# Expert inputs fetched by rows with an indirect DMA and transposed, in place of one-hot products; eight weight buffers in place of five

## The chip, the core and the metric

One core of a Trainium2 chip runs the whole kernel in one launch. The metric is the device time in microseconds of one execution. Engines are named as in the profile: PE (TensorE, the matrix engine), DVE (VectorE), ACT (ScalarE), POOL (GpSimd), SP (SyncE, which here only issues DMAs). Transfers between the chip's DRAM and the on-chip SBUF run on 16 DMA engines, whichever engine issues them.

## What is computed

Two transformer blocks over 512 tokens of width 1024, everything in float32. The first block (two layers with recurrence, retention and spatial gating) and the attention of the second are not touched. The second block ends in a mixture of 32 experts, of which each token takes 4:

```python
def moe_ffn(h, w_router, b_router, w_gate_up, b_gate_up, w_down, b_down):
    logits = jnp.dot(h, w_router) + b_router
    top_logit, top_idx = lax.top_k(logits, TOP_K)        # TOP_K = 4 of N_EXPERTS = 32
    gate = jax.nn.softmax(top_logit, axis=-1)
    ...
    def expert_block(args):
        tok, g, e = args
        xb = h_pad[tok]                                  # rows of the tokens of expert e
        gu = xb @ w_gate_up[e] + b_gate_up[e]            # 1024 -> 2 x 1024
        y = clamped_swiglu(gu) @ w_down[e] + b_down[e]   # 1024 -> 1024
        return y * g[:, None]
    ...
    out = jnp.zeros((n_tok + 1, d), y.dtype).at[slot_tok].add(y.reshape(n_slots, d))
```

Then `x + gt2 * moe_ffn(h2)` is normalized and written out. An expert has a matrix of 1024 x 2048 and one of 1024 x 1024, 12 MB; 32 of them are 384 MB, each read once.

## The kernel before

Products run in a 1-pass float32 format of the matrix engine. To keep the accuracy, each operand is split into a high and a low part: ACT copies the value into the short format (`hi`), DVE subtracts that from the value (`lo`), both in `split` (L278 to L280), and a product is the sum of three, hi x hi, lo x hi and hi x lo.

The first 1.27 ms are the dense part; the expert stage follows. It starts with `router` (L1020 to L1149): logits, the choice of four, the position of each pair among those of its expert (`pos`), and four values per pair (`vals`: token, filled, gate in two parts). Its last loop (L1136 to L1148) makes the scaled and shifted rows of the tokens in four quarters of 256 columns, `raw`, and splits each into `hn` (two tiles, 16 KB per partition each), where all rows stay in SBUF for the whole stage.

`moe` (L1468) then goes through the experts in order. One expert has up to 128 slots (`CAP`). `gate_up(e, hf)` makes one half of the gate columns (`pg`) and of the linear ones (`pl`) in four weight tiles, each with 12 products of 512 columns; `act_rows` transposes the activations of a half (4 transposes by PE, then a split); `down(e, hf)` multiplies them with two tiles of the second matrix (`pd`). Order: `gate_up(e, 0)`, `down(e-1, 1)`, `gate_up(e, 1)`, `down(e, 0)`. Behind `down(e, 1)` the result is scaled by the gate and `accumulate` (L1213) adds its rows to `x_rows` in DRAM, an indirect DMA issued by POOL; empty slots have an index out of bounds and move nothing.

`gather(e0)` (L1281) prepares the inputs of two experts, e0 and e0+1. DVE makes a one-hot matrix `oh` (512 tokens x 256 slots) from `pos`; PE multiplies both parts of all rows with it: for each of 4 pairs of 128-column chunks and each of 2 parts, 8 products of 256 columns into one PSUM tile `xT`, which ACT copies into `x`, already transposed. Then a small product with `vals` ("slot") and two small transposes ("slotT") give the token index and the gate of each slot (`slot_columns`, L1200). It is a generator with four parts; `moe` calls the next part in the last tile (t == 3) of each `gate_up`, so that the inputs for experts e+2 and e+3 are made while e and e+1 run. Gather 0 runs ahead of the loop.

`wsplit` (L1218) loads one weight tile of 1 MB (128 x 2048 f32) with a DMA issued by SP and splits it. The landing tiles take turns in five buffers (`wsts`, i % 5), the hi and lo tiles in three each. A scheduler orders the instructions of each engine when the program is built, by priorities and its own estimates; on the chip each engine runs them in that order and waits on semaphores.

Of the kernel before, what the change touches and what calls it, by code (L numbers as in the profile page):

```python
# [26 lines left out]
# ------------------------------------------------------------------ layout  # L27
# [27 lines left out]
# order in which the column chunks of w_in are used: LRU input, LRU gate, retention, spatial gating  # L55
# [101 lines left out]
    # experts: [e][tile][p][...] with each tile one run per partition; four tiles of two row chunks for each  # L157
    # half of the gate columns beside the like half of the linear ones, then four tiles of w_down
# [6 lines left out]
    # constants of the shapes  # L165
# [26 lines left out]
# ------------------------------------------------------------------ kernel  # L192

class Kern:
# [6 lines left out]
    # tiles of one tag are handed out in program order, so each role has its own  # L201
# [16 lines left out]
    # ---- weights of the dense part, in the order of their use; splits run ahead as far as the buffers reach  # L218
# [43 lines left out]
    def weights(self, key, m=128, held=0):  # L262
        """the next weights, (hi, lo); held: how many before them are still in use"""
# [19 lines left out]
    # ---- 1 / sqrt(x * scale + eps) of a few columns, by Newton steps  # L283
# [14 lines left out]
    def colsum(self, *sq, nblk=4):  # L298
        """sum over partitions of [128, nblk * 128] -> PSUM [128 (token in block), nblk]"""
# [7 lines left out]
    def bcast(self, nat, out, nblk=4, p=None):  # L307
        """[128 (token in block), nblk] -> [128, nblk * 128], every partition the same row"""
# [6 lines left out]
    def row_bcast(self, cols, out):  # L315
        """[128, 8] columns of a feature vector -> two [128, 512], every partition the vector"""
# [27 lines left out]
    def lru_scale(self):  # L344
        """-8 * softplus(-lambda), and 4 * softplus(-lambda)"""
# [23 lines left out]
    def rope_tables(self):  # L369
        """cos and signed sin of positions * inv, [128, T], both halves of the head alike"""  # L370
# [31 lines left out]
    # ---- rms norm of self.h: y = h * g split; 1 / rms goes in where products leave PSUM  # L402
# [25 lines left out]
    def square_sum(self, ss, h, k, scale=1.0, n=T):  # L428
        """ss = sum over k of (h * scale) ** 2"""
# [8 lines left out]
    def proj(self, w, y, nk=DC, p=None, between=()):  # L438
        """one chunk of 128 output features for all tokens -> PSUM; between: what goes between its products"""
# [8 lines left out]
    def projs(self, keys, y, ws=()):  # L448
        """three chunks side by side, so that none waits for the last rows of y; ws: weights that are there"""
# [8 lines left out]
    def silu_gate(self, l, c, y, rs):  # L458
        """g * sigmoid(g) of chunk c"""
# [8 lines left out]
    def gated(self, o, gs):  # L468
        """o * gs, split"""
# [5 lines left out]
    # ---- recurrent branch, group g of three chunks  # L475
    def lru_group(self, l, g, y, rs):
# [41 lines left out]
        # sqrt(1 - a^2) = (1 + a) sqrt(tanh(-log(a) / 2))  # L518
# [13 lines left out]
    def rope(self, p, hi, lo, tabs):  # L532
        """rotated chunk, split"""
# [11 lines left out]
    # ---- retention branch, heads 2 * hp and 2 * hp + 1  # L545
# [72 lines left out]
    # ---- spatial gating branch  # L618
# [73 lines left out]
    def layer(self, l):  # L692
# [32 lines left out]
        # per-layer embedding  # L725
# [35 lines left out]
    # ---- block 2: modulation of both conditions, as columns; each call is half the rows for 512 columns  # L761
# [37 lines left out]
    def modcols(self, name, gain, j, o):  # L799
        """gain * (1 + scale); scale is the modulation of condition j at column o"""  # L800
# [6 lines left out]
    def modulated(self, src, a, b, bc, t, yh, yl):  # L807
        """(src * a) * bc + b, split; a and b are columns"""
# [6 lines left out]
    def headnorm(self, p, n):  # L815
        """1 / rms over the 128 features of a head -> [128, n] rows"""
# [7 lines left out]
    def context(self):  # L824
        """modulated context, split"""
# [20 lines left out]
    def context_kv(self):  # L846
        nc = self.nc
        # keys of a head: (hi, lo) of the tokens, then (hi, lo) of the context; values: six blocks of keys
# [36 lines left out]
    def block2(self):  # L885
# [3 lines left out]
        # final norm of block 1 and first norm of block 2: with A = mean(h^2) + eps, the product of both  # L889
        # 1 / rms is 1 / sqrt(mean((h g)^2) + eps A)  # L890
# [16 lines left out]
        # tables of the axial rotation with the gains of q and k  # L907
# [19 lines left out]
        # short convolution; the scores of the first head between its last products  # L927
# [29 lines left out]
        # attention  # L957
# [13 lines left out]
    def scores(self, q, kv, P, early=False):  # L971
        """softmax of one head: four blocks of queries by rows, keys (tokens, context)"""
# [46 lines left out]
    # ---- second norm, router, slots of the experts; stops before each chunk of the residual and at the end  # L1019
    def router(self):  # L1020
# [10 lines left out]
        # bias of the logits: b_router + w_router.T @ shift  # L1031
# [13 lines left out]
        # triangle and ones for the counts, and four columns that stand for the choices beyond the fourth  # L1045
# [9 lines left out]
        for k in range(8):  # L1055
# [12 lines left out]
            # tokens by rows  # L1068
# [31 lines left out]
        # choices of the tokens  # L1100
# [3 lines left out]
        # position of each pair among those of its expert  # L1104
# [176 lines left out]
    def gather(self, e0):  # L1281
# [8 lines left out]
        for j in range(4):  # L1290
# [12 lines left out]
            if j < 3:  # L1303
                yield
# [359 lines left out]
```

## Time and profile before

| | |
|---|---|
| median of three runs | 2576.26 us (2575.6 to 2578.38) |
| profiled execution, first to last instruction | 2573.3 us |
| PE busy | 2521.1 us, 98% |
| DVE busy | 2030.0 us, 79% |
| ACT busy | 1403.1 us, 55% |
| POOL busy | 145.4 us, 6% |
| DMA | 553.92 MB, mean 215 GB/s |
| clock granted to PE, mean | 0.994 of full speed |

The profile lists instructions with the line that made them, the tile written and the tiles read. "PEld" is the load of a product's fixed operand and runs beside the products. Busy times of neighbouring matrix products overlap, since they are pipelined; how fast they follow each other is seen in their start times. A line can be that of a helper: all splits stand under L279 (ACT) and L280 (DVE), so they are told apart by their tiles. The stage of the experts begins at about 1270 us, and from about 1320 to 2540 us every pair of experts looks alike.

### The profile page before, as it was taken

How to read it: one execution, taken by the hardware profiler on the slowest of the kernel's cores; microseconds unless marked ns; L12 is line 12 of the kernel's file. 1: busy time of each engine (PE TensorE's matmuls, PEld its weight loads, DVE VectorE, ACT ScalarE, POOL GpSimd, SP SyncE). 2: the span in 40 equal slices, each digit the busy share in tenths (PEclk: the TensorE clock that was granted, in tenths of full speed). 3: DMA queues.
4: the chain of work that ended last, by engine and by line, in shares of the span. 5: the costliest groups of instructions: out<-in, count | busy, mean ns of one | idle time of the engine just before them, and what ended most of it. 6: DMA issues, size and time to landing. Idle time of an engine off the chain costs nothing. (4 is left out here: it accounts for less than half of the span.)

```text
span 2573.3 us, 31850 instructions
## 1 busy us (share of the span) xinstructions
PE 2521.1 (98%) x12331; PEld 2042.9 (79%) x12331; DVE 2030.0 (79%) x2582; ACT 1403.1 (55%) x1469; POOL 145.4 (6%) x85
## 2 busy tenths in 40 slices
PE   8999999999999999999899999999999999999997
PEld 6778878777788787887678888888888888888885
DVE  8866757578576577868788888888888888888897
ACT  6523324345233245334666666666666666666665
POOL 0000000000000000000210101101001011010013
PEclk9999999999999999999899999999999999999998
DMA  4243242422423433220288888888898888888886
GB/s 161 82 142 99 82 163 95 139 97 90 153 83 101 162 118 131 66 92 17 107 325 335 320 334 316 324 338 318 324 330 320 331 318 317 338 327 317 330 325 242
DMA packets 104525, 553.92 MB, mean 215 GB/s; under 512 B 13872, under 2 KB 14256, under 8 KB 55216
## 3 DMA queue, kind: packets, MB, share of 16 engines
q1 hardware_dynamic: 94368, 532.85, 56.7%
q0 software_dynamic: 5248, 10.64, 2.0%
q10 hardware_dynamic: 4752, 8.34, 1.0%
q8 instruction: 99, 1.62, 0.3%
q14 instruction: 58, 0.48, 0.1%
HBM read 539.18 MB, written 20.97 MB: 218 GB/s over the span
## 5 line engine op out<-in xcount | busy, mean ns | idle before, releaser
L279 ACT ACTIVATE wh<-w 128x2048 fp32r<-128x2048 f32 (+2 forms) x571 | 923.3, 1619 | 694.5 <-PE pd L1375 196.5
L280 DVE TENSOR_TENSOR wl<-w,wh 128x2048 fp32r<-128x2048 f32 (+2 forms) x571 | 1092.8, 1924 | 223.1 <-ACT wh L279 221.1
L1335 PE MATMUL pg<-wh,x 128*128 128x512 f32 x1024 | 411.0, 401 | 0.0
L1336 PE MATMUL pl<-wh,x 128*128 128x512 f32 x1024 | 404.8, 395 | 0.0
L274 PE MATMUL prj<-ty,wh 128*128 128x512 f32 x880 | 349.6, 397 | 11.3 <-ACT wh L279 8.5
L275 PE MATMUL prj<-ty,wh 128*128 128x512 f32 x880 | 347.7, 395 | 1.1 <-DVE ty L812 0.8
L276 PE MATMUL prj<-ty,wl 128*128 128x512 f32 x880 | 346.4, 394 | 1.1 <-DVE wl L280 1.1
L1335 PEld LDWEIGHTS pg<-wh,x 128*128 128x128 f32 x1024 | 192.7, 188 | 44.6 <-ACT x L1300 0.7
L1336 PEld LDWEIGHTS pl<-wh,x 128*128 128x128 f32 x1024 | 192.8, 188 | 43.0
L1335 PE MATMUL pg<-wl,x 128*128 128x512 f32 x512 | 202.8, 396 | 1.9 <-DVE wl L280 1.9
L274 PEld LDWEIGHTS prj<-ty,wh 128*128 128x128 f32 x880 | 166.4, 189 | 48.1 <-ACT wh L279 9.8
L1336 PE MATMUL pl<-wl,x 128*128 128x512 f32 x512 | 202.2, 395 | 0.0
L276 PEld LDWEIGHTS prj<-ty,wl 128*128 128x128 f32 x880 | 166.2, 189 | 37.9 <-DVE wl L280 2.5
L275 PEld LDWEIGHTS prj<-ty,wh 128*128 128x128 f32 x880 | 166.1, 189 | 35.7 <-DVE ty L812 1.8
L1215 POOL DMA_INDIRECT x_rows<-ye,si x32 | 105.3, 3292 | 1123.5 <-DVE ye L1383 1123.5
L1375 PE MATMUL pd<-wl,ah 128*128 128x512 f32 x512 | 165.6, 400 | 0.0
L1375 PE MATMUL pd<-wh,al 128*128 128x512 f32 x512 | 161.7, 397 | 0.0
L1375 PE MATMUL pd<-wh,ah 128*128 128x512 f32 x512 | 161.1, 396 | 0.0
L274 PE MATMUL prj<-tmix,wh 128*128 128x512 f32 x320 | 127.1, 398 | 0.4 <-ACT tmix L279 0.4
L275 PE MATMUL prj<-tmix,wh 128*128 128x512 f32 x320 | 126.5, 395 | 0.0
L276 PE MATMUL prj<-tmix,wl 128*128 128x512 f32 x320 | 126.0, 394 | 0.0
L1335 PEld LDWEIGHTS pg<-wl,x 128*128 128x128 f32 x512 | 96.3, 188 | 26.1 <-DVE wl L280 2.7
(440 smaller groups left out, 3736.3 us busy)
## 6 DMA issues: line engine op xcount, KB each, us to landing
w<-in_wgu SPq DMA_DIRECT2D x256, 1024.0 KB, 5.4
w<-in_wdn SPq DMA_DIRECT2D x128, 1024.0 KB, 7.0
w<-in_w SPq DMA_DIRECT2D x118, 512.0 KB, 3.4
wa<-in_wada SPq DMA_DIRECT2D x48, 512.0 KB, 3.4
w<-in_wob SPq DMA_DIRECT2D x32, 384.0 KB, 3.1
w<-in_wg SPq DMA_DIRECT2D x16, 512.0 KB, 3.5
w<-in_wos SPq DMA_DIRECT2D x8, 512.0 KB, 3.3
w<-in_wo SPq DMA_DIRECT2D x8, 512.0 KB, 3.3
```

Source lines behind the costliest of these rows:

```text
L274: mm(ps, a[0], b[0], start=first, stop=False)
L275: mm(ps, a[0], b[1], start=False, stop=False)
L276: mm(ps, a[1], b[0], start=False, stop=last)
L279: ins = self.nc.scalar.activation(hi, src, AF.Copy).ins
L280: self.nc.vector.tensor_sub(lo, src, hi.bitcast(F32))
L1215: self.nc.gpsimd.indirect_dma_start(out=self.x_d[:, :], out_offset=self.rows(idx), in_=y, in_offset=None, bounds_check=T - 1, oob_is_err=F ...
L1335: nc.tensor.matmul(pg, x[k], w[:, s, 0], start=first, stop=False)
L1336: nc.tensor.matmul(pl, x[k], w[:, s, 1], start=first, stop=False)
L1375: nc.tensor.matmul(self.pd[n], a[:, k], w[:, s, n * 512:(n + 1) * 512], start=hf == 0 and k == 0 and a is ah and w is wh, stop=hf == 1 and ...
```

## The change

All scaled rows go to DRAM: in `router`, each quarter of `raw` is stored into `h_rows` and no longer split, and `hn` is gone. `gather(e0)` first makes the slots' indices and gates, then POOL issues two indirect DMAs that fetch the rows of each expert, 4 KB per filled slot, into two landing tiles `xg` (zeroed once; an empty slot keeps what it held). The next two parts, one for each expert, transpose its rows with PE in two groups of four 128x128 blocks, and `split` makes the two parts from PSUM (ACT and DVE). The one-hot matrix stays for the indices. The generator has three parts in place of four, and in `moe` the calls for the first two experts are as for the others, from the second half of expert 0 on. In the space of `hn` stand three more landing buffers for weights: eight in turn (i % 8). In `overflow`, which runs only where an expert has over 128 pairs, the rows need not be put together again. Comments and doc strings are cut too.

```diff
@@ router
             for b in range(0 if j else 4):
-                nc.scalar.activation(r[:, b], r[:, b], AF.Copy, scale=nat[:, b:b + 1])
+                self.scaled = nc.scalar.activation(r[:, b], r[:, b], AF.Copy, scale=nat[:, b:b + 1]).ins
...
-                ins = self.split(r, *(x[:, :, j * 256:j * 256 + 256] for x in self.hn))
-            if j == 0:
-                self.scaled = ins
+            nc.sync.dma_start(self.h_d.rearrange("(b p) c -> p b c", p=128)[:, :, j * 256:j * 256 + 256], r)
@@ rows_pools
-        rows = self.ctx.enter_context(pool("mrows", 1))
-        self.hn = [rows.tile([128, 4, D], F32R, name=f"hn{x}") for x in "hl"]
-        self.wsts = [self.moe_pools.enter_context(pool("mw", 1))]
+        self.xgp = self.moe_pools.enter_context(pool("mxg", 2))
+        self.wsts = 3 * [self.moe_pools.enter_context(pool("mwa", 3))]
+        self.wsts += [self.moe_pools.enter_context(pool("mw", 1))]
@@ wsplit
-        w = self.wsts[i % 5].tile([128, 2048], F32, name="w", tag="w", bufs=3 if 0 < i % 5 < 4 else 1)
+        w = self.wsts[i % 8].tile([128, 2048], F32, name="w", tag="w", bufs=1 if i % 8 in (3, 7) else 3)
@@ gather
+        ahead = 0 if e0 else AHEAD
+        xg = []
+        for q in range(2):
+            xg.append(self.xgp.tile([128, D], F32, name="xg", tag="xg"))
+            if e0 == 0:
+                nc.gpsimd.memset(xg[q], 0.0)
+        with tc.high_priority(ahead):
             self.hot = nc.vector.tensor_tensor(oh, ...
...            (slot, slotT and slot_columns, moved here from the end)
+                nc.gpsimd.indirect_dma_start(out=xg[q], out_offset=None, in_=self.h_d[:, :],
+                                             in_offset=self.rows(self.idx[e0 + q]),
+                                             bounds_check=T - 1, oob_is_err=False)
+        yield
         for q in range(2):
             self.xs[e0 + q] = [], []
-        for j in range(4):
-            for i in range(2):
-                p = self.trp("xT")
-                for s in range(2):
-                    k = 2 * j + s
-                    for b in range(4):
-                        nc.tensor.matmul(p[:, s * 256:(s + 1) * 256], self.hn[i][:, b, k * 128:(k + 1) * 128], oh[:, b],
-                                         start=b == 0, stop=b == 3)
-                t = (self.xp if e0 % 4 else self.hpool).tile([128, 2, 2, 128], F32R, name="x", tag="h", bufs=8)
-                with self.tc.high_priority(0 if e0 else AHEAD):
-                    nc.scalar.activation(t.rearrange("p s q c -> p (s q c)"), p, AF.Copy)
-                for q in range(2):
-                    self.xs[e0 + q][i].extend(t[:, s, q] for s in range(2))
-            if j < 3:
-                yield
+            with tc.high_priority(ahead):
+                for hf in range(2):
+                    p = self.trp("xT")
+                    for k in range(4):
+                        c = (4 * hf + k) * 128
+                        nc.tensor.transpose(p[:, k * 128:(k + 1) * 128], xg[q][:, c:c + 128], self.ident)
+                    pool = self.xp if e0 % 4 else self.hpool
+                    t = [pool.tile([128, 4, 128], F32R, name="x", tag="h", bufs=8) for _ in range(2)]
+                    self.split(p.rearrange("p (k s) -> p k s", k=4), *t)
+                    for i in range(2):
+                        self.xs[e0 + q][i].extend(t[i][:, k] for k in range(4))
+            yield
@@ moe
-                    for _ in range((t == 3) * (0, 1, 2, 1)[2 * e + hf] if e < 2 else t == 3):
+                    if t == 3 and e + hf:
                         next(g, None)
```

## Rows read from the trace of the kernel before

**Rows 1.** The page's chain that ended last: shares of the span by line.
```profile
PE pd L1375 14%; PE pg L1335 14%; PE pl L1336 14%; PE xT L1296 4%; PE aT L1359 1%; PE pl L1339 1%; PE pg L1339 1%; PE slot L1307 0%; PE slotT L1313 0%; DVE xr L1436 0%; DVE wl L280 0%; ACT fsq L1423 0%; DVE xr L1422 0%; DVE rx L290 0%; PE fx L1419 0%
```
**Rows 2.** Busy times, one pair: length, engines (instructions), PE clock, DMA share, GB/s.
```profile
1716.00:1795.00 79.00, 79.00 (x383) 64.74 (x382) 69.01 (x51) 53.87 (x42) 6.70 (x2) 1.00 0.89 326
```
**Rows 3.** Instructions of ACT in order (start, duration): the slot copy, three pairs apart.
```profile
1438.63 0.36 ACT L1310 ACTIVATE slr<-slot 8x256 f32<-8x256 f32 x1
...
1676.15 0.36 ACT L1310 ACTIVATE slr<-slot 8x256 f32<-8x256 f32 x1
```
**Rows 4.** Instructions of PE in order, merged runs counted: transposes, products, one gather call.
```profile
1707.22 0.60 PE L1359 MATMUL aT<-ident,li 128*128 128x128 f32 x4
1707.58 0.48 PE L1335 MATMUL pg<-wh,x 128*128 128x512 f32 x1
1707.89 0.40 PE L1336 MATMUL pl<-wh,x 128*128 128x512 f32 x1
...
1713.03 0.40 PE L1336 MATMUL pl<-wl,x 128*128 128x512 f32 x1
1713.26 1.07 PE L1296 MATMUL xT<-oh,hnh 128*128 128x256 f32 x8
1714.17 1.07 PE L1296 MATMUL xT<-oh,hnl 128*128 128x256 f32 x8
1715.08 0.39 PE L1339 MATMUL pg<-bias,sel 128*128 128x512 f32 x1
```
**Rows 5.** Groups by line and shape, 1300 to 2540: busy us, mean ns, idle before.
```profile
L280 DVE TENSOR_TENSOR wl<-w,wh 128x2048 fp32r<-128x2048 f32 x376 | 857.5, 2294 | 141.4 <-ACT wh L279 139.9
...
L280 DVE TENSOR_TENSOR al<-aT,ah 128x512 fp32r<-128x512 f32 x63 | 43.1, 684 | 0.4 <-ACT ah L279 0.4
```
**Rows 6.** Waits of the engines, 1300 to 2540: total us, times, longest.
```profile
ACT wh L279 <- PE pd L1375: 196.5, 123, 3.0
ACT wh L279 <- PE pl L1336: 187.2, 247, 2.0
DVE wl L280 <- ACT wh L279: 139.9, 236, 2.5
```
**Rows 7.** Waits of SP's DMA queue, 1300 to 2540: total us, times, longest.
```profile
SPq L1222 <- DVE wl L280: 1044.1, 359, 7.8
```
**Rows 8.** Instructions of DVE and of POOL in order, about an accumulation.
```profile
1743.56 6.71 DVE L280 TENSOR_TENSOR wl<-w,wh 128x2048 fp32r<-128x2048 f32 x3
...
1743.92 3.35 POOL L1215 DMA_INDIRECT x_rows<-ye,si  x1 [35.73 <-DVE ye L1383]
```
**Rows 9.** DMA issues with median us to landing; then the index tile's DMAs.
```profile
x_rows<-hr POOLq DMA_DIRECT2D x4, 512.0 KB, 4.7
x_rows<-ye,si POOLq DMA_INDIRECT x32, 10.9
...
DMA to landing us min/median/max: 6.3/10.9/13.0
```
**Rows 10.** Busy times in stretches of 5 us; the last two: DMA share, GB/s.
```profile
1725.00:1730.00 5.00, 5.00 (x26) 4.03 (x25) 4.45 (x3) 3.28 (x4) 0.00 (x0) 1.00 1.00 400
...
1750.00:1755.00 5.00, 5.00 (x33) 4.17 (x32) 4.14 (x4) 4.12 (x5) 0.00 (x0) 1.00 1.01 282
```
**Rows 11.** The start: DVE and PE in order of time; a stretch with the clock.
```profile
1272.99 0.40 DVE L1127 TENSOR_TENSOR vals<-tE,vals 128x128 fp32r<-128x128 f32 x1
1274.44 1.67 DVE L1145 SCALAR_TENSOR_TENSOR raw<-raw,nat,tF 128x256 f32<-128x256 f32 x4
...
1276.51 0.63 PE L1335 MATMUL pg<-wh,x 128*128 128x512 f32 x1
...
1287.40 0.63 PE L1307 MATMUL slot<-oh,vals 128*8 128x256 f32 x4
...
1290.76 0.17 DVE L1206 TENSOR_SCALAR si<-st 128x2 int32<-128x2 f32 x1
...
1270.00:1275.00 5.00, 3.07 (x13) 2.73 (x13) 4.96 (x17) 3.12 (x5) 0.00 (x0) 0.50 0.02 5
```

More of the change, by code (lines that the diff above doesn't have):

```diff
@@ L1281, in gather @@
     def gather(self, e0):
-        nc = self.nc
+        nc, tc = self.nc, self.tc
+        ahead = 0 if e0 else AHEAD
         oh = self.work2.tile([128, 4, 2, 128], F32R, name="oh", tag="oh")
         S = [128, 4, 2, 128]
-        with self.tc.high_priority(0 if e0 else AHEAD):
+        xg = []
[4 more added lines that the diff above has]
+        with tc.high_priority(ahead):
@@ L1286, in gather @@
             self.hot = nc.vector.tensor_tensor(oh, self.rt[:, None, None, 292:420].to_broadcast(S),
                                                self.pos[:, :, e0:e0 + 2, None].to_broadcast(S), op=OP.is_equal).ins
+            p = self.trp("slot")
+            for b in range(4):
+                nc.tensor.matmul(p[:8, :256], self.vals[:, b, e0:e0 + 2].rearrange("p e c -> p (e c)"), oh[:, b],
+                                 start=b == 0, stop=b == 3)
+            st = self.work2.tile([128, 440], F32, name="slr", tag="slr", bufs=1)[:, :256]
@@ new lines, in gather @@
+            nc.scalar.activation(st[:8], p[:8, :256], AF.Copy)
+            p = self.trp("slotT")
+            for q in range(2):
+                nc.tensor.transpose(p[:, q * 8:q * 8 + 8], st[:8, q * 128:(q + 1) * 128], self.ident[:8, :8])
+            sl = self.work2.tile([128, 2, 4], F32, name="slc", tag="slc", bufs=2)
+            for q in range(2):
+                nc.vector.tensor_copy(sl[:, q], p[:, 12 * q:12 * q + 4])
+            idx, gate = self.slot_columns(self.work2, sl, 2)
+            for q in range(2):
+                self.idx[e0 + q], self.gate[e0 + q] = idx[:, q:q + 1], gate[:, q:q + 1]
+                nc.gpsimd.indirect_dma_start(out=xg[q], out_offset=None, in_=self.h_d[:, :],
+                                             in_offset=self.rows(self.idx[e0 + q]),
+                                             bounds_check=T - 1, oob_is_err=False)
@@ L1288, in gather @@
+        yield
         for q in range(2):
             self.xs[e0 + q] = [], []
-        for j in range(4):
-            for i in range(2):
-                p = self.trp("xT")
-                for s in range(2):
-                    k = 2 * j + s
-                    for b in range(4):
-                        nc.tensor.matmul(p[:, s * 256:(s + 1) * 256], self.hn[i][:, b, k * 128:(k + 1) * 128], oh[:, b],
-                                         start=b == 0, stop=b == 3)
-                t = (self.xp if e0 % 4 else self.hpool).tile([128, 2, 2, 128], F32R, name="x", tag="h", bufs=8)
-                with self.tc.high_priority(0 if e0 else AHEAD):
-                    nc.scalar.activation(t.rearrange("p s q c -> p (s q c)"), p, AF.Copy)
-                for q in range(2):
-                    self.xs[e0 + q][i].extend(t[:, s, q] for s in range(2))
-            if j < 3:
-                yield
@@ L1305, in gather @@
-        p = self.trp("slot")
-        for b in range(4):
-            nc.tensor.matmul(p[:8, :256], self.vals[:, b, e0:e0 + 2].rearrange("p e c -> p (e c)"), oh[:, b],
-                             start=b == 0, stop=b == 3)
-        st = self.work2.tile([128, 440], F32, name="slr", tag="slr", bufs=1)[:, :256]
-        nc.scalar.activation(st[:8], p[:8, :256], AF.Copy)
-        p = self.trp("slotT")
-        for q in range(2):
-            nc.tensor.transpose(p[:, q * 8:q * 8 + 8], st[:8, q * 128:(q + 1) * 128], self.ident[:8, :8])
@@ L1314, in gather @@
-        sl = self.work2.tile([128, 2, 4], F32, name="slc", tag="slc", bufs=2)
-        for q in range(2):
-            nc.vector.tensor_copy(sl[:, q], p[:, 12 * q:12 * q + 4])
-        idx, gate = self.slot_columns(self.work2, sl, 2)
-        for q in range(2):
-            self.idx[e0 + q], self.gate[e0 + q] = idx[:, q:q + 1], gate[:, q:q + 1]
-        yield
+            with tc.high_priority(ahead):
[9 more added lines that the diff above has]
+                        self.xs[e0 + q][i].extend(t[i][:, k] for k in range(4))
@@ L1400, in finish @@
         nc, d = self.nc, self.d
-        gf = self.wsts[4].tile([128, 2048], F32, name="gf", tag="w", bufs=1)[:, :D]
+        gf = self.wsts[7].tile([128, 2048], F32, name="gf", tag="w", bufs=1)[:, :D]
         nc.sync.dma_start(gf, bass.AP(tensor=d["gfin"].tensor, offset=d["gfin"].offset, ap=[[0, 128], [1, D]]))
@@ L1455, in expert_bias @@
         nc.gpsimd.memset(self.sel.bitcast(F32), 0.0)
-        st = self.wsts[0].tile([128, 2048], F32, name="bst", tag="w", bufs=1)[:, :1024]
+        st = self.wsts[3].tile([128, 2048], F32, name="bst", tag="w", bufs=1)[:, :1024]
         one = self.const.tile([128, 1], F32, name="one")
@@ L1524, in overflow @@
                 wk = c.enter_context(tc.tile_pool(name="ow", bufs=1))
-                for b in range(4):
-                    hr = wk.tile([128, D], F32, name="hr", tag="oy")
-                    nc.vector.tensor_add(hr, self.hn[0][:, b].bitcast(F32), self.hn[1][:, b].bitcast(F32))
-                    nc.sync.dma_start(self.h_d[b * 128:(b + 1) * 128], hr)
                 g2 = wk.tile([128, D], F32, name="og2")
```

## The prediction

> **What bounds the kernel now.** I read the chain of waits first. Its shares by line are matrix products of the expert stage: the three product lines L1375, L1335 and L1336 hold 14% each, and L1296, the one-hot products that this change removes, holds 4% [rows 1]. The reader is to see that no wait, no DMA and no other engine has a share of that size. Next I read the busy times over one pair of experts: in 79.00 us PE is busy for 79.00, DVE for 69.01, ACT for 53.87 and POOL for 6.70; the DMA engines are 0.89 busy at 326 GB/s, with the clock at 1.00, its 2.4 GHz level [rows 2]. The length of a pair comes from a copy that runs once per pair: from 1438.63 to 1676.15 there are three, so (1676.15 - 1438.63) / 3 = 79.17 us [rows 3]. A busy PE need not be a dense one, so I read the start times: from 1707.89 to 1713.03 there are 22 intervals of 0.2336 us without a hole [rows 4]. PE is full. Last come the waits: ACT waits for PE to give back split buffers (196.5 and 187.2 us in 1240), DVE for ACT (139.9) [rows 6], and the queue that loads weights waits for DVE to empty a buffer (1044.1 us) [rows 7]. So every stage ahead of PE is waiting for PE: in this stage a microsecond less of PE is a microsecond less of time, until the next resource is full. The three candidates lie close: DVE has 10 us of idle time per pair, DMA 11% of its time.
>
> **The one-hot products go.** Per pair the old gather has four calls, each with 16 products of 256 columns. In the row view one call runs from 1713.26 to 1715.08: 1.82 us [rows 4]. Four make 7.28 us per pair. The row and gate columns (products "slot" and "slotT") stay; they only move to the front.
>
> **The transposes come.** Per pair there are 2 experts x 2 halves x 4 = 16 transposes of 128x128 f32, in groups of four. The same group exists already for the activations: it starts at 1707.22, the next product starts at 1707.58, and that one takes 0.31 instead of 0.2336 until its follower [rows 4]. A group costs 0.36 + 0.08 = 0.44 us, four of them 1.76. PE saves 7.28 - 1.76 = 5.52 us per pair and goes to 79.17 - 5.52 = 73.65. There are 15 such pairs in the stage (the gathers for experts 2 to 30); the gather for experts 0 and 1 is costed with the start. 15 x 5.52 = 82.8 us.
>
> **DVE gets work.** Each half row is now split in high and low parts, where before ACT alone copied it: 4 subtractions from PSUM per pair, like the "al" of 684 ns [rows 5], 2.74 us. DVE goes to about 69.2 + 2.7 = 71.9 us of 73.65. That is 98% by busy time; the busy times of neighbours overlap a little (three weight subtractions take 6.71 us together [rows 8] where three single ones would take 3 x 2.294 = 6.88 [rows 5]), so it is somewhat less. DVE is covered by PE, but barely. The queue is strictly in order, and the weight tile that stands behind a new subtraction is PE's next food. I allow 0.3 us of PE stall per pair, 5 us in all; the bounds are 0 (all hidden) and 1.85 (DVE itself sets a pair of about 75.5). ACT makes 4 copies instead of 8 per pair and has 25 us to spare: nothing.
>
> **The indirect DMA.** Its nearest row is the indirect accumulation of an expert's output, with the same shape and the same index columns: 3.35 us on POOL [rows 8] and 6.3 to 13.0 us from issue to landing, 10.9 in the median [rows 9]. POOL has 72 us idle per pair, so two more take nothing there by themselves; behind them on POOL stands only the accumulation, whose result nobody needs before the end. Who waits is PE: its transposes stand in a fixed order. The index call now comes at the end of one half expert and the first transposes at the end of the next. Between them lie 74 products and one transposed group: 74 x 0.2336 + 0.44 = 17.7 us. From the slot product to the finished indices it takes 3.5 us (1287.40 to 1290.93 [rows 11]); with 10.9 more the rows are there at 14.4, with 13.0 at 16.5. Both are earlier than 17.7: no wait. The second expert's rows are issued 3.35 us later and needed 18 us later. Cover is 1.2 to 3.3 us; if it is gone, each microsecond costs 15 in all.
>
> **Bytes.** Each pair reads 128 rows of 4 KB more, 0.52 MB (512 tokens x 4 choices / 32 experts = 64 rows in the mean). Loads run at 400 GB/s at a share of 1.00 when nothing else is under way, and at 282 beside an accumulation [rows 10]. The cheap bound is 0.52 MB / 400 = 1.3 us per pair. The dear bound treats a gather like an accumulation: (400 - 282) / 400 x 10.9 = 3.2 us, so 6.4 us per pair. The DMA engines are now busy for 0.89 x 79.17 = 70.5 us per pair, so afterwards 71.8 to 76.9 against PE's 73.65. I take the cheap side, as a gather has no read of its target. The three more weight buffers cost no time: they let loads run ahead, and smooth what the gathers disturb.
>
> The Trainium skill speaks against this at one point. "DMA: Bandwidth & Descriptors", section Bandwidth, says that for HBM to SBUF the HBM side binds, at about 358 GB/s per core. By it a pair (25.17 MB of weights, 0.52 gathered, 0.52 accumulated) would take 73.2 us, or 74.6 if the accumulation's reads are counted: an estimate from the page, level with PE. The trace here does not agree with it as a ceiling, as the 400 GB/s show [rows 10].
>
> **The start.** Here the change adds a wait. Before, the products of expert 0 start at 1276.51, fed by one-hot products as the scaled rows come. Now all rows must first be scaled, stored, and fetched again. The gates end at 1272.99 + 0.40 = 1273.39; then 12 scalings of 1.67 / 4 = 0.42 us make 5.0 us: 1278.4 [rows 11]. The store of the last quarter (512 KB, as the old store of rows: 4.7 us [rows 9]): 1283.1. The fetch, 6.3 to 10.9: 1289.4 to 1294.0, and I lean to the short end, because the weight buffers are full by then and the engines idle. Transposes at the lower clock (0.50 of full speed, its 1.2 GHz level, as in the trace now after the idle time [rows 11]), copy and subtraction: 0.7 + 0.58 + 0.68 = 2.0. First product at 1291 to 1296, 15 to 19.5 us late. Back come six of the eight groups of 8 one-hot products that now lie between the first products: 6 x 0.91 = 5.5. Net 9.5 to 14 us; I take 11. The range is 0 (waits of DVE on the residual that now fall into the idle time) to 20 (the store is issued by SP, which also issues the weight loads in order, and a load that waits for a buffer would hold it). The two fills of the landing tiles on POOL lie in its idle time ahead of the router's end. The end of the kernel is untouched: the last gather is two experts earlier.
>
> **Sum.** The profiled span is 2573.3 and the median of the runs 2576.26; the 3 us outside are not touched, so the differences go onto the median. 2576.3 - 82.8 + 5 + 11 = 2509.5, say 2510.
>
> **The rivals.**
> - DMA becomes the bound. For: 0.89 busy already. Against: the loads wait 1044 us for buffers [rows 7], so the queue is held back and not full. A pair of 74 to 76.9 us gives 2576.3 - 15 x (79.17 - 74 or 76.9) + 11 = 2510 to 2553. Chance 0.17.
> - DVE becomes the bound, a pair of 74.5 to 75.5: 2517 to 2532. Chance 0.09.
> - The fetched rows come up to 4.4 us after PE asks for them, in each pair: 2510 to 2575. Chance 0.07.
> - The same wait, larger, is the case on the other side. Place: the first transposes of each pair in PE's order. It decides from 5.2 - 11/15 = 4.5 us of lateness on, that is when landing takes over 17.7 - 3.5 + 4.5 = 18.7 us. If landing doubles to 21.8 because gathers, accumulation and eight loads share the engines, PE stands 7.6 us per pair: 2576.3 + 15 x (7.6 - 5.2) + 11 = 2623. For: 10.9 is measured with five loads in the buffers. Against: no landing above 13.0 [rows 9]. Chance 0.08.
> - POOL's indirect DMAs hold up DVE. If each stopped DVE for its 3.35 us, two more would bring DVE to 71.9 + 6.7 = 78.6 per pair and eat the gain: 2576.3 - 15 x 0.6 + 11 = 2578. Against: three weight subtractions beside one take 2.24 us each [rows 8], no more than the mean of all, 2.294 [rows 5]. Chance 0.02. "SBUF — State Buffer" of the Trainium skill, section "SBUF: two separate sides", says that DVE with two SBUF inputs and a GpSimd operation that reads SBUF exclude each other for the whole instruction; by the same rows that does not hold for these.
>
> **How the numbers follow.** The forecast (PE stays the bound, 2494 to 2528) has 0.57. The range 2494 to 2552 takes in the DMA and DVE cases and the smaller half of the late rows; outside lie the large lateness, the port case and a start that costs nothing. A measurement of this kernel can tell about 0.2% (5 us) from no change: faster 0.89, the same 0.03, slower 0.08.
>
> **What would show it.** Right: no one-hot products, 16 transposes per pair, a pair of 73.7 to 74.5 us with PE without holes, DVE at 95% or more, weight loads that wait less. Wrong: waits of the transposes for the gather's landing; waits of products for the low weight parts with DVE full; waits of ACT's weight copies for the loads, with a DMA share of 1; a first product of expert 0 after 1300.

## The result

The changed kernel takes 2705.32 us (median of 4 runs, 2701.95 to 2709.74) against 2576.91 us before: a ratio of 1.0499, 95% interval [1.0485, 1.0513]. It was forecast at 2510; it became 5% slower. The profiled execution spans 2708.0 us, where before spanned 2573.3: 134.7 us more.

The page of the changed kernel, busy times and the shares of the chain that ended last:

```profile
PE 2495.3 (92%) x11563; PEld 1979.1 (73%) x11563; DVE 2049.2 (76%) x2642; ACT 1366.0 (50%) x1401; POOL 221.6 (8%) x119
...
PE 3%; DVE 1%; issue 1%; DMA 0%; ACT 0%; DVEq 0%; POOLq 0%; ACTq 0%
PE pg L1340 1%; PE pl L1341 1%; PE pd L1380 1%; DVE wl L280 0%; DMA xg<-h_rows,si 0%; DVE wl L1229 0%; DVE ye L1388 0%; DMA x_rows<-ye,si 0%; DVE li L1351 0%; DVE xr L1441 0%; PE xT L1319 0%; ACT fsq L1428 0%; PE pl L1344 0%; PE pg L1344 0%; DVE xr L1427 0%
```

PE has lost the work that it was meant to lose (2521.1 us busy before, 12331 instructions: 1024 products fewer and 256 transposes more are 11563). But PE no longer fills the span. The chain can't be used here as in [rows 1]: it was followed only through the last few per cent of the span. What it does pass through is telling all the same: DMAs of `xg` and of `x_rows`, which had no share before.

Busy times of the stretch 1400 to 2480 (length, then PE, PEld, DVE, ACT, POOL, then PE clock, DMA share, GB/s), first of before, then of the changed kernel:

```profile
1400.00:2480.00 1080.00, 1080.00 (x5209) 884.67 (x5208) 943.56 (x689) 736.56 (x558) 90.46 (x27) 1.00 0.88 325
```

```profile
1400.00:2480.00 1080.00, 951.62 (x4065) 744.32 (x4064) 860.62 (x661) 631.00 (x450) 132.48 (x50) 0.93 0.81 297
```

Every engine but POOL is busy for less, and so are the DMA engines: nothing is full any more. The time went into waiting. Where [rows 2] showed PE busy for all of its time, PE now idles for 128 of 1080 us.

The waits of DVE and then of PE in the changed kernel, 1300 to 2660 (total us, times, longest):

```profile
DVE si L1204 <- DMA x_rows<-ye,si: 46.8, 8, 6.9
...
DVE si L1204 <- issue: 21.0, 6, 6.6
...
PE xT L1319 <- DMA xg<-h_rows,si: 65.4, 14, 11.7
PE pg L1340 <- DVE wl L280: 54.6, 31, 5.9
```

Before had none of the first three, and 1.7 us of the last (1300 to 2540). DVE stops 14 times at `si`, the 128x2 tile of token indices, for 4.8 us in the mean and up to 6.9, and the stage makes indices 15 times in this stretch. For the six stops under "issue" the profile names no releaser; they too end 6.6 to 10.8 us after POOL began an accumulation. PE stops at the transposes for the fetched rows, and at products for a low weight part.

One pair shows how these hang together. DVE, POOL and PE of the changed kernel in order of time (start, duration, and in brackets the idle time before and what ended it):

```profile
1395.65 0.15 DVE L1205 TENSOR_TENSOR sg<-slc 128x2 f32<-128x2 f32 x1
1395.72 2.28 DVE L280 TENSOR_TENSOR wl<-w,wh 128x2048 fp32r<-128x2048 f32 x1
1404.90 0.17 DVE L1204 TENSOR_SCALAR si<-st 128x2 int32<-128x2 f32 x1 [6.90 <-DMA x_rows<-ye,si]
...
1393.82 3.34 POOL L1213 DMA_INDIRECT x_rows<-ye,si  x1 [33.34 <-DVE ye L1388]
1405.85 2.93 POOL L1308 DMA_INDIRECT xg<-h_rows,si  x1 [8.70 <-issue]
...
1407.91 0.80 PE L1340 MATMUL pg<-wl,x 128*128 128x512 f32 x1 [5.89 <-DVE wl L280]
1408.51 0.63 PE L1341 MATMUL pl<-wl,x 128*128 128x512 f32 x1
1408.93 0.63 PE L1340 MATMUL pg<-wh,x 128*128 128x512 f32 x1
...
1414.96 0.45 PE L1319 MATMUL xT<-ident,xg 128*128 128x128 f32 x1 [3.41 <-DMA xg<-h_rows,si]
```

POOL issues the accumulation of an expert's output at 1393.82. It takes its rows' addresses from an index tile, and the program gives that tile back only when the DMA has landed. There are two such tiles in turn. The index part, now at the front of `gather`, wants to write the next indices while the accumulation of the pair before last is still under way with the same buffer. DVE, whose instructions run in order, stands from 1398.0 to 1404.90. Behind `si` stand the weight subtractions: PE runs out of low weight parts at about 1402.0 and waits 5.89 us. And the fetch, which needs the indices, is issued only at 1405.85, so PE stops once more for its rows, 3.41 us.

### The profile page after: what moved, and what is told of

Read it like the earlier page. It is cut to its first block, busy times and chain, and to the rows that moved or that the text cites. A ratio compares the mean times of both kernels' runs of the same rounds, so it can differ in the third digit from the quotient of the medians.

```text
span 2708.0 us, 30486 instructions
## 1 busy us (share of the span) xinstructions
PE 2495.3 (92%) x11563; PEld 1979.1 (73%) x11563; DVE 2049.2 (76%) x2642; ACT 1366.0 (50%) x1401; POOL 221.6 (8%) x119
## 5 line engine op out<-in xcount | busy, mean ns | idle before, releaser
L1340 PE MATMUL pg<-wl,x 128*128 128x512 f32 x512 | 214.9, 420 | 60.9 <-DVE wl L280 55.0
L274 PEld LDWEIGHTS prj<-ty,wh 128*128 128x128 f32 x880 | 166.2, 189 | 48.9 <-ACT wh L279 10.7
L1213 POOL DMA_INDIRECT x_rows<-ye,si x32 | 97.6, 3051 | 1050.8 <-DVE ye L1388 1043.5
L1380 PE MATMUL pd<-wh,ah 128*128 128x512 f32 x512 | 175.4, 422 | 0.0
L1340 PEld LDWEIGHTS pg<-wl,x 128*128 128x128 f32 x512 | 98.4, 192 | 99.9 <-DVE wl L280 72.6
L1380 PE MATMUL pd<-wh,al 128*128 128x512 f32 x512 | 168.1, 410 | 0.0
L1319 PE MATMUL xT<-ident,xg 128*128 128x128 f32 x256 | 55.3, 342 | 83.3 <-DMA xg<-h_rows,si 83.3
L1380 PEld LDWEIGHTS pd<-wl,ah 128*128 128x128 f32 x512 | 97.7, 195 | 45.4 <-DVE wl L280 21.9
L274 PE MATMUL prj<-tmix,wh 128*128 128x512 f32 x320 | 127.0, 398 | 0.4 <-ACT tmix L279 0.4
```

The source lines that it names most:

```text
L1213: self.nc.gpsimd.indirect_dma_start(out=self.x_d[:, :], out_offset=self.rows(idx), in_=y, in_offset=None, bounds_check=T - 1, oob_is_err=F ...
L1319: nc.tensor.transpose(p[:, k * 128:(k + 1) * 128], xg[q][:, c:c + 128], self.ident)
L1340: nc.tensor.matmul(pg, x[k], w[:, s, 0], start=first, stop=False)
L1380: nc.tensor.matmul(self.pd[n], a[:, k], w[:, s, n * 512:(n + 1) * 512], start=hf == 0 and k == 0 and a is ah and w is wh, stop=hf == 1 and ...
```

## The experiments

Theory A: the time is lost because the index part writes the index tile while the accumulation of the pair before last still uses it; DVE stops, and with it the weights and the fetch. Rivals: the fetch itself (its transfers, POOL's work, its landing) is what costs; the gate tile of the same part is what holds; the three more weight buffers disturb.

**E1: a third buffer for the small tiles.**

```diff
-        t = pool.tile([128, n], F32, name="st", tag="st", bufs=2)
-        idx = pool.tile([128, n], I32, name="si", tag="si", bufs=2)
-        gate = pool.tile([128, n], F32, name="sg", tag="sg2", bufs=2)
+        t = pool.tile([128, n], F32, name="st", tag="st", bufs=3)
+        idx = pool.tile([128, n], I32, name="si", tag="si", bufs=3)
+        gate = pool.tile([128, n], F32, name="sg", tag="sg2", bufs=3)
```

> The changed kernel with three buffers in place of two for the small tiles of the slots (token index, gate, intermediate). Theory A: in the changed kernel the index of a pair is written early, into the tile that the last accumulation of the pair before last still reads, so DVE stands in its order until that accumulation has landed; with a third buffer the wait goes, a pair of experts takes 73.7 to 74.5 us and the time is 2515 to 2535 (the start stays about 18 us late). Theory B: the fetched rows are late because gathers, accumulations and eight loads share the DMA engines; the index tiles don't matter, a pair stays at 86 to 88 us and the time at 2690 to 2710. Theory C: DVE is too full with the added subtractions; the third buffer gives part, a pair of 76 to 80 us, 2550 to 2620.

Measured: 2540.91 us (2538.25 to 2542.95), ratio to before 0.986 [0.9843, 0.9876]: 164 us less than the changed kernel, and 1.4% less than before. That is 6 us above the range expected by theory A, 9 below that of C, and 149 below that of B. The same stretch of E1:

```profile
1400.00:2480.00 1080.00, 1060.59 (x4762) 843.23 (x4762) 995.57 (x766) 736.04 (x526) 180.74 (x54) 1.00 0.94 346
```

E1's waits of PE for the fetched rows, 1320 to 1700, where all that are left lie (DVE has none at `si`):

```profile
PE xT L1319 <- DMA xg<-h_rows,si: 10.0, 3, 4.3
```

And its slot copy on ACT, once per pair, nine pairs apart:

```profile
1692.01 0.37 ACT L1298 ACTIVATE slr<-slot 8x256 f32<-8x256 f32 x1 [1.87 <-PE slot L1295]
...
2368.20 0.38 ACT L1298 ACTIVATE slr<-slot 8x256 f32<-8x256 f32 x1 [1.87 <-PE slot L1295]
```

The waits of `si` are gone, and with them nearly all waits for the rows, though the rows take the same way. A pair takes (2368.20 - 1692.01) / 9 = 75.13 us, where [rows 3] had 79.17.

**E1b and E1c: the index tile alone, and the other two alone.**

```diff
 E1b
-        idx = pool.tile([128, n], I32, name="si", tag="si", bufs=2)
+        idx = pool.tile([128, n], I32, name="si", tag="si", bufs=3)
 E1c
-        t = pool.tile([128, n], F32, name="st", tag="st", bufs=2)
+        t = pool.tile([128, n], F32, name="st", tag="st", bufs=3)
-        gate = pool.tile([128, n], F32, name="sg", tag="sg2", bufs=2)
+        gate = pool.tile([128, n], F32, name="sg", tag="sg2", bufs=3)
```

> As the run before, but only the index tile has three buffers; the gate and the intermediate keep two. Theory A in its narrow form (the landing of the accumulation, which reads the index alone): all of the gain is here, 2515 to 2540. If the gate tile counts too, because it can be written only after DVE has scaled the output of the pair before last, part is left: 2540 to 2620. Theory B: no gain, about 2700.

> The changed kernel with three buffers for the gate and the intermediate tile, and two for the index. With the run that has three for the index alone it tells the two tiles apart. If the landing of the accumulation (index tile) is the larger part: 2640 to 2700. If the gate tile, which fixes the index part behind the scaling of an output, is the larger part: 2560 to 2620.

Measured, one run each: 2626.93 us with the index tile alone, 2704.55 with the other two alone; each is 5 to 7 us above the nearest range expected. The other two alone are worth nothing: DVE still waits 68.0 us at `si` (1300 to 2660), where the changed kernel has 67.8. The index tile alone is worth 78 of the 164 us, and the other two, once it is there, the remaining 86. DVE and POOL with the index tile alone, one pair:

```profile
1794.08 0.16 DVE L1204 TENSOR_SCALAR si<-st 128x2 int32<-128x2 f32 x1
1794.33 1.41 DVE L1388 SCALAR_TENSOR_TENSOR ye<-pd,sg,g 128x512 f32<-128x512 f32 x2
...
1797.86 0.16 DVE L1205 TENSOR_TENSOR sg<-slc 128x2 f32<-128x2 f32 x1
...
1795.02 1.06 POOL L1308 DMA_INDIRECT xg<-h_rows,si  x1 [38.13 <-PE pd L1380]
```

`si` waits for nothing now, but it stands late in DVE's order, right ahead of `ye`, and the gate sum `sg` has to stand behind `ye`, which reads the gate tile of the pair before last. The fetch goes out at 1795.02, and PE waits for rows 12 times (47.3 us in 1300 to 2660). So there are two holds on the index part, the accumulation's (index tile) and that of `ye` (gate tile); the second shows only when the first is gone, and is then worth as much. The gate tile and the intermediate `st` were not tried apart; of the two only the gate tile is read by `ye`. Why the order puts `si` so late in E1b isn't shown by the trace.

**E7: the old kernel, with only the index part moved to the front.** Nothing is fetched; the one-hot products stay.

```diff
@@ gather (kernel before)
             (oh)
+        (slot, slotT, slot_columns: two buffers, as before)
         for j in range(4):
             (one-hot products)
-        (slot, slotT, slot_columns)
```

> The kernel before, one-hot products and five weight buffers, with one thing moved: the index part stands first in a gather, as in the changed kernel, and its small tiles keep two buffers. No transfer is added. Theory A (the index is written into a tile that an accumulation still reads): DVE stands once per pair for up to 7 us, PE starves behind it by about 4 us per pair, 2610 to 2670. Theory B (the fetched rows are the trouble): the same as before, 2571 to 2582.

Measured: 2621.69 us, ratio 1.0171 [1.0154, 1.0188]: 45 us slower than before. DVE's waits at `si`, 1400 to 2480:

```profile
DVE si L1206 <- DMA x_rows<-ye,si: 91.3, 14, 8.5
```

DVE and POOL in one pair of E7:

```profile
1729.79 0.17 DVE L1206 TENSOR_SCALAR si<-st 128x2 int32<-128x2 f32 x1 [6.66 <-DMA x_rows<-ye,si]
1729.86 0.69 DVE L280 TENSOR_TENSOR al<-aT,ah 128x512 fp32r<-128x512 f32 x1
...
1718.93 3.34 POOL L1215 DMA_INDIRECT x_rows<-ye,si  x1 [36.68 <-DVE ye L1383]
```

The same wait, once per pair, 6.5 us in the mean, in a kernel without any fetch. So the move by itself costs, and the fetch isn't needed for it. PE stops here at the one-hot products, which wait for DVE's `al`, the instruction right behind `si` (PE's waits, 1400 to 2480):

```profile
PE xT L1311 <- DVE al L280: 29.6, 12, 4.0
```

That only 45 of the 91 us reach the end fits that DVE had 10 us of idle time per pair [rows 2]. With the fetch behind it the same hold costs more, the 164 us of E1: PE then waits for the rows themselves (65.4 us) and for low weight parts (54.6 us).

**E4: the index part half an expert later, two buffers.**

```diff
-                    if t == 3 and e + hf:
+                    if t == 3 and (e % 2 or hf):
```

> The changed kernel with two buffers as it is, but the index part of a gather is called one half expert later, behind the accumulation whose tile it takes over. Theory A: that accumulation has been issued 11 us or more earlier and has landed, so the wait is gone or short, 2515 to 2550. Theory B: no gain, since the rows are asked for later still and needed later by the same amount, 2690 to 2710.

Measured: 2547.69 us, ratio 0.9883 [0.9864, 0.9903]. The second cure has nothing to do with buffers, only with when the tile is written, and brings 158 of the 164 us.

**E9: both cures.** The three buffers of E1, and

```diff
-                    if t == 3 and e + hf:
+                    if t == 3 and (e % 2 or hf):
```

> Both cures at once: three index, gate and sum buffers, and the index part half an expert later. If the wait for a free index tile is the whole cause, one cure makes the other superfluous: the index tile is free by the time the later index part writes it, so the third buffers change nothing against the later index part alone (2547.7), within 4 us. If the later place with two buffers still held something up, the third buffers would bring it to 2541 or below.

Measured: 2532.29 us (2530.4 to 2535.39), ratio 0.9829 [0.9812, 0.9845]; it is the second case of the expectation, as the first, no change against E4 within 4 us, missed by 15 us. The waits of DVE at `si` in E4, 1300 to 2660:

```profile
DVE si L1204 <- DMA x_rows<-ye,si: 7.2, 2, 5.8
...
DVE si L1204 <- issue: 1.8, 1, 1.8
```

Three of its 15 pairs still wait, 9 us in all; in E9 none does. Along with these waits PE's own for `wl` at `pd` shrink, from 13.4 us in E4 to 3.8 in E9; the rest of the 15 us isn't accounted for. Half an expert later is nearly late enough, not quite. This is the fastest version that computes everything: 1.7% faster than before. Its slot copies, ten pairs apart:

```profile
1624.26 0.37 ACT L1298 ACTIVATE slr<-slot 8x256 f32<-8x256 f32 x1 [0.86 <-PE slot L1295]
...
2371.89 0.37 ACT L1298 ACTIVATE slr<-slot 8x256 f32<-8x256 f32 x1 [0.87 <-PE slot L1295]
```

A pair takes (2371.89 - 1624.26) / 10 = 74.76 us.

**E2: E1 with five landing buffers for weights, as before.**

```diff
-        self.wsts = 3 * [self.moe_pools.enter_context(pool("mwa", 3))]
-        self.wsts += [self.moe_pools.enter_context(pool("mw", 1))]
+        self.wsts = [self.moe_pools.enter_context(pool("mw", 1))]
...
-        w = self.wsts[i % 8].tile(...)
+        w = self.wsts[i % 5].tile(...)
```

> Three buffers for the small tiles, and five weight buffers as in the kernel before. It tells what the three more weight buffers are worth once the wait is gone. If PE stays the bound with five, it is the same as with eight within 5 us. If gathers disturb the loads so that they need to run ahead, it is 15 to 60 us slower than with eight.

Measured: 2548.63 us, ratio 0.9893 [0.9876, 0.991]: 7.7 us more than E1, between the two cases expected. The three more buffers are worth something, and they don't disturb. In the changed kernel they were not tried apart; there, while DVE stands, no buffer is emptied, and the DMA share falls to 0.17 in 1404 to 1408.

**E6: E1 without the 30 later fetches.**

```diff
-                nc.gpsimd.indirect_dma_start(out=xg[q], ...)
+                if e0 == 0:
+                    nc.gpsimd.indirect_dma_start(out=xg[q], ...)
```

> Three buffers for the small tiles, and the rows are fetched only for experts 0 and 1; all other experts transpose the rows that these two left, which leaves 30 fetches out of the computation. It tells the price of those fetches. If they are hidden: within 5 us of the run with three buffers (2536 to 2546). If their transfers or their lateness cost, it is 10 to 40 us faster than that.

Measured: 2529.01 us, ratio 0.9809 [0.9793, 0.9825]. The 30 later fetches together cost 12 us in E1, near the low end of the second case expected, and not 164. Busy times, 1720 to 2020, of E1 and of E6:

```profile
1720.00:2020.00 300.00, 295.75 (x1336) 235.06 (x1335) 279.54 (x216) 205.20 (x148) 55.27 (x16) 1.00 0.96 350
```

```profile
1720.00:2020.00 300.00, 295.78 (x1335) 235.49 (x1334) 280.01 (x216) 205.07 (x149) 35.62 (x8) 1.00 0.94 343
```

PE's busy time in these four pairs is the same to 0.03 us. In the steady pairs a fetch is free, although the DMA engines are 0.96 busy; the 12 us lie in the first pairs, where E1 has its three waits for rows (10.0 us): from the accumulation of expert 0 to that of expert 8 E6 takes 1654.07 - 1356.47 = 297.6 us, E1 1668.80 - 1357.20 = 311.6.

**E5: E1 with four pairs of split buffers (and six landing buffers).** E1 was 31 us over the forecast, with PE waiting for `wl` for some tenths of a microsecond at a time.

```diff
-            self.whs = [first, self.early, self.early]
-            self.wls = [first, self.work2, self.work2]
+            self.whs = [first, self.early, self.early, self.mwa]
+            self.wls = [first, self.work2, self.work2, self.mwa]
```

> Three buffers for the small tiles, and the space of two landing buffers given to a fourth pair of high and low weight tiles (six landing buffers, four split ones). What is left over PE's own 73.65 us per pair, some 1.5 us, shows as waits of products for the low weight parts. If these come from DVE being late by less than a tile now and then, a fourth pair takes them up: a pair of 73.7 to 74.2 us, 2518 to 2532. If DVE or the loads are the bound on average, it is the same, 2536 to 2550.

Measured: 2543.1 us, ratio 0.9864 [0.9847, 0.988], the same as E1, and PE's waits for `wl` stay (13.7 us in 1300 to 2660, 13.1 in E1). It isn't for want of split buffers that the low parts come late. The two landing buffers given up for them may hide a small gain, as E2 lost 7.7 us with three fewer.

**E8: E1 with the four subtractions for the fetched rows taken from DVE.**

```diff
-                    self.split(p.rearrange("p (k s) -> p k s", k=4), *t)
+                    for i in range(2):
+                        nc.scalar.activation(t[i], p.rearrange("p (k s) -> p k s", k=4), AF.Copy)
```

> The changed kernel with three index buffers, and the low part of the fetched rows is not computed: ACT makes a second copy in its place (part of the arithmetic is left out), so that DVE has four operations of 0.68 us less in each pair (2.7 us) and ACT four copies of 0.59 us more. The matrix products are the same in number and shape. If what is left over the forecast in the steady pairs (75.15 us where 73.65 to 73.95 were expected) comes from DVE, which has hardly any idle time left and so delivers low weight parts late, a pair falls to 73.6 to 74.1 us and the time to 2518 to 2528. If it comes from the products themselves, from the transfers or from the fetch, a pair stays at 75.1 us and the time within 5 us of 2541.

Measured: 2520.93 us (2520.76 to 2522.97), ratio 0.9784 [0.9767, 0.98]: 20 us less than E1, inside the range that went with DVE. But the pairs don't follow: the slot copy comes at 1599.12 and, ten pairs later, at 2346.08, which is 74.70 us each, 0.43 less than in E1, where 1.0 to 1.5 were expected. Most of the gain lies in the first four pairs: from the accumulation of expert 0 to that of expert 8 E8 takes 1650.60 - 1354.30 = 296.3 us, E1 311.6. PE has no wait for rows left in E8, and E6, which has no fetches there, gains about as much in these pairs; so most of the gain goes with rows that come in time. What DVE's load costs in a steady pair isn't settled, as E8 also gives ACT more work; nor is what keeps a steady pair at 74.7 us and not 73.65, with DVE busy for 273.48 of 300 us. PE still waits for `wl` (7.4 us in 18 places, 1700 to 2420) while DVE waits for ACT's weight copies (63.8 us in 60 places, 1300 to 2480) and for PE (33.0 us in 39 places at `li`), which points to the fixed orders of the engines; no run tested that.

## Why the prediction was wrong, step by step

To set the pieces side by side I take one event that all kernels have, the accumulation of an expert's output on POOL: that of expert 0 ends the start, that of expert 28 comes 14 pairs later. Rows of POOL, first before, then the changed kernel, E1 and E9:

```profile
1348.63 2.88 POOL L1215 DMA_INDIRECT x_rows<-ye,si  x1 [37.81 <-DVE ye L1383]
...
2456.49 3.35 POOL L1215 DMA_INDIRECT x_rows<-ye,si  x1 [35.72 <-DVE ye L1383]
```

```profile
1357.07 3.41 POOL L1213 DMA_INDIRECT x_rows<-ye,si  x1 [11.84 <-DVE ye L1388]
...
2587.35 3.42 POOL L1213 DMA_INDIRECT x_rows<-ye,si  x1 [31.85 <-DVE ye L1388]
```

```profile
1357.20 3.41 POOL L1213 DMA_INDIRECT x_rows<-ye,si  x1 [11.82 <-DVE ye L1388]
...
2420.72 5.56 POOL L1213 DMA_INDIRECT x_rows<-ye,si  x1 [34.30 <-DVE ye L1388]
```

```profile
1356.09 3.41 POOL L1213 DMA_INDIRECT x_rows<-ye,si  x1 [11.81 <-DVE ye L1388]
...
2408.05 5.62 POOL L1213 DMA_INDIRECT x_rows<-ye,si  x1 [26.27 <-DVE ye L1388]
```

Against before, in us (the forecast has one of its 15 pairs, 5.2 us, in the first column; the end is the span less the second row of each fence):

| | to expert 0 | 14 pairs | from expert 28 to the end | sum |
|---|---|---|---|---|
| forecast | +5.8 | -72.6 | 0 | -66.8 |
| changed kernel | +8.4 | +122.4 | +3.8 | +134.7 |
| E1 | +8.6 | -44.3 | +3.7 | -32.1 |
| E9 | +7.5 | -55.9 | +4.3 | -44.1 |

- **The one-hot products go, the transposes come: right.** The instruction counts above agree. A group of four transposes with E8's rows starts at 1711.05, the next product at 1711.41 and its follower at 1711.72: 0.36 + 0.08 = 0.44 us, as taken from the activations' group [rows 4].
- **"The row and gate columns (...) stay; they only move to the front": this is the step that failed.** The move was costed at nothing, and the hold that it makes is worth 164 of the 195 us missed, the changed kernel against E1. The prediction followed the new fetch through POOL and the DMA queues, but not the small tiles that the moved part writes. Before, the index part ran after `down(e-1, 1)` and the accumulation of expert e-1; moved to the end of `gate_up(e, 0)`, it stands ahead of `down(e-1, 1)`, whose `ye` reads the gate tile and whose accumulation reads the index tile, both of the pair whose buffers it wants to write. So on the chip `sg` had to come behind that `ye`, and `si` behind the landing of that accumulation. The rows needed for it were there: the accumulation's place in [rows 8], its landing of 6.3 to 13.0 us in [rows 9]. What was missing was the question, for each tile written by the moved part, who reads it last and when that is over. E7 shows the price of the move alone (45 us), E1 that with free tiles DVE has no wait at `si` left.
- **The fetch: right where its indices are in time.** Its landing is 8.5 us in the median of the changed kernel, less than the 10.9 taken; E1 has three waits for rows in all. The rival of late rows named the right place, PE's transposes (65.4 us of waits), with the wrong cause: not a long landing but a late issue. Its price, 2623, was also too small, as it held no DVE that stands.
- **DVE: the size was off, then the allowance.** 71.9 us per pair was forecast; E1 has 279.54 / 300 x 75.13 = 70.0, since neighbours overlap more than I allowed: DVE's single times add up to 2.2 us per pair more than its busy time before, and to 3.8 more in E1 (1400 to 2480). Yet the stall that I put at 0.3 us per pair is 75.13 - 73.65 = 1.5 in E1 and 1.1 in E9. "Covered, but barely" by busy time says little when two engines with fixed orders wait for each other.
- **Bytes: right.** With the fetches E1 moves 350 GB/s at a share of 0.96, without them E6 343 at 0.94, at the same pace; 0.96 x 75.13 = 72.1 us per pair, near the cheap side's 71.8. The rate of 358 GB/s that the Trainium skill gives in "DMA: Bandwidth & Descriptors", section Bandwidth, was no ceiling here: E8 moved 366 GB/s from 1320 to 1420. The same section gives it as what each core gets with both cores of a pair streaming, which the prediction left out. (The prediction's 74.6 us, with the accumulation's reads, comes to 74.7.)
- **The start: right.** The first product of expert 0 comes at 1297.81 in the changed kernel, 21.3 us after that of [rows 11], of which 2.8 lie in the router ahead; the remaining 18.5 are in the forecast range of 15 to 19.5. Net it is +8.4 against +5.8.
- **The end: not untouched.** About 4 us are lost there in the changed kernel, E1 and E9, but 1.7 in E2 (2546.6 - 2428.14 = 118.5, before 2573.3 - 2456.49 = 116.8); the last section has the rows that bear on it.
- **The range.** The miss is 195 us, with every rival of the prediction priced below 2625. None of them had DVE stopped by a tile in use, so no width worked out from them could have held it.

## What to carry to other kernels

When a block of small instructions is moved forward, go through every tile that it writes, find the last reader of the buffer it will get, and ask when that reader is done; for a DMA the end is its landing, not its issue. On an engine that runs in order, one waiting 128x2 instruction holds everything behind it, so its price is that of the work behind it (here PE's next weights) and not its own 0.17 us. A third buffer of a few bytes turned a loss of 5% into a gain of 1.4%, a place half an expert later into one of 1.2%, and both together into one of 1.7%.

## What the runs showed of the hardware

**The index tile of an indirect DMA came free only with its landing.** The accumulation takes 3.3 us on POOL, but the index tile came free 11.1 us after the start of the instruction (1393.82 to 1404.90), and the landing of these DMAs is 10.7 us in the median of the changed kernel (1300 to 2640). This is when the program's wait ends; whether the DMA still reads the tile so late isn't shown.

**After a stop of 5.89 us PE ran at about half speed for some 3 us.** Busy times in stretches of 4 us about the wait at 1402 to 1408 in the changed kernel; the last three columns are clock, DMA share and GB/s:

```profile
1400.00:1404.00 4.00, 2.02 (x9) 1.30 (x7) 0.00 (x0) 1.91 (x1) 0.00 (x0) 1.00 0.89 275
1404.00:1408.00 4.00, 0.09 (x1) 0.09 (x1) 3.10 (x4) 0.00 (x0) 2.15 (x1) 0.55 0.17 72
1408.00:1412.00 4.00, 3.55 (x8) 2.40 (x8) 4.00 (x2) 1.07 (x1) 2.66 (x2) 0.59 0.77 262
...
1420.00:1424.00 4.00, 4.00 (x19) 3.22 (x18) 3.67 (x3) 2.31 (x2) 0.00 (x0) 1.00 0.07 8
```

PE idles from 1402.0 to 1407.91. The granted clock is 1.00, the 2.4 GHz level, in the stretch where it stops, and 0.55 and 0.59 in the two behind it, near the 1.2 GHz level; products then start 0.42 to 0.43 us apart (1408.51 and 1408.93) in place of 0.2336 [rows 4]. So this wait cost more than its length: the eight products behind it lost some 1.5 us.

**DVE is held by POOL's arithmetic, though not by its indirect DMAs.** The last weight tiles are split half by DVE, half by POOL (L1229). POOL and DVE at the end of E1:

```profile
2504.24 5.50 POOL L1229 TENSOR_TENSOR wl<-w,wh 128x1024 fp32r<-128x1024 f32 x2 [8.25 <-ACT wh L1228]
...
2521.89 5.48 POOL L1430 TENSOR_TENSOR xr<-xr,gf 128x512 f32<-128x512 f32 x4
...
2503.45 1.22 DVE L1229 TENSOR_TENSOR wl<-w,wh 128x1024 fp32r<-128x1024 f32 x1
...
2505.30 2.19 DVE L1353 SCALAR_TENSOR_TENSOR li<-sg,sig,li 128x512 f32<-128x512 f32 x1
2507.41 3.41 DVE L1229 TENSOR_TENSOR wl<-w,wh 128x1024 fp32r<-128x1024 f32 x1
...
2523.56 3.84 DVE L1432 TENSOR_TENSOR fms<-fms 128x2 f32<-128x2 f32 x1
```

The same subtraction takes DVE 1.22 us ahead of POOL's and 3.41 beside them; it ends at 2510.82, about 1.1 us after POOL's second one (2504.24 + 5.50 = 2509.74). The product with `sg` takes 2.19 us, where the same operation takes 0.746 in the mean of the other pairs. Here the rule of the Trainium skill ("SBUF — State Buffer", section "SBUF: two separate sides"), that a DVE operation with two SBUF inputs and a GpSimd operation that reads SBUF exclude each other, agrees with the rows; beside indirect DMAs [rows 8] spoke against it. In before DVE has one such long row among the last weights, in E1 three, some 4.5 us more in all. They aren't the whole loss at the end: E2 has the same three (2.17, 3.41 and 3.01 us) and loses 1.7 us. E1's other 2 us lie behind its last `ye`, where DVE's `fms` takes 3.84 us beside POOL's `xr`; in before and in E2 it takes 0.33. Whether these rows are the cause was not tried.
